# Seventeen expert products in fp32, dealt out through the choice of experts

## The chip, the cores and the metric

The kernel runs on one core of a Trainium2 chip. A core has TensorE (PE in the profile, with PEld for its weight loads), VectorE (DVE), ScalarE (ACT), GpSimd (POOL) and SyncE (SP), which here only issues transfers. The metric is the device time of one execution in microseconds.

## What is computed

Three transformer blocks stand behind one another, for 256 tokens of width 1024. The change lies in the first block, in a layer with 16384 small experts. Of the reference, this is what matters:

```python
def peer_ffn(h, w_q, sub_keys, u_tab, v_tab):          # h: 256 tokens x 1024
    q = (xt @ w_q).reshape(n_tok, 8, 2, 128)
    s = jnp.einsum('thpk,pnk->thpn', q, sub_keys)      # 8 heads x 2 halves x 128 keys
    top_s, top_i = lax.top_k(s, 16)
    cand_s = top_s[:, :, 0, :, None] + top_s[:, :, 1, None, :]   # 16 x 16 sums
    cand_i = top_i[:, :, 0, :, None] * 128 + top_i[:, :, 1, None, :]
    best_s, best_pos = lax.top_k(cand_s, 16)
    experts = take_along_axis(cand_i, best_pos)        # 16 experts per head and token
    gates = softmax(best_s)
    hid = gelu(einsum(u_tab[experts], x))              # one number per chosen expert
    return einsum(gates * hid, v_tab[experts])
...
e = (p @ ple_w_proj) * sigmoid(h @ ple_w_gate + ple_b_gate)
x = layer_norm(alpha * h + f + e)
```

## The kernel before

No expert is gathered. The kernel computes the up product of all 16384 experts for all tokens, weights the results with a coefficient that is zero for experts that a token did not choose, and multiplies by the whole down table. The up table is cut into 64 chunks of 256 experts (one transfer of 1 MB each), the down table likewise.

A product in this kernel is usually made of three matmuls in fp32r: the fp32 weight is split into `hi` (an ACT copy, line 319) and `lo` = weight - `hi` (a subtraction, line 320), the activations likewise, and `mm3` (lines 328 to 332) adds hi x hi, hi x lo and lo x hi. `wsplit` (line 308) loads a chunk into one of four `raw` buffers through SP's queue and splits it in two halves of 1024 columns. While `aside` is set, the subtraction goes to GpSimd and not to VectorE.

One up product, `Experts.up(j)` (line 943), takes one of two `mm` banks of PSUM: 2 x 8 times `mm3`, 48 matmuls, and a Gelu eviction into one of 18 `gel` tiles (line 951). Up products 0 to 17 can therefore run before any down product; each later one waits until `down` has freed a `gel`.

The stage `chosen` (line 855) runs in this order. Eight chunks of queries and scores give the sixteen best keys of each half (`top16`). Two up products follow, with their subtractions on GpSimd. Then `route` (line 779) is called for each of two tiles of 128 tokens: on VectorE it forms the 50 candidate sums that can matter, takes their sixteen best for each of 8 heads (lines 800 to 801), the softmax, and then, eight times, compares 16 positions with 50 candidates (`eq`, line 818), multiplies by the candidates' codes (line 820) and adds up (line 821). GpSimd forms the codes (lines 784 to 796). Three transposes on TensorE (`c.transpose`, line 469) and three ACT copies (line 831) put expert rows, columns and gates into `eT` and `gT`. `best`, `posf`, `ei` and `ef` have one buffer each, so the second tile's choice rewrites them only when the first one's transposes have read them.

The coefficient loop (lines 883 to 898) has 64 groups of four tokens. VectorE makes one `bm` (a one-hot of columns for four tokens, line 888) and four `am` (a one-hot of rows times the gate, line 894), TensorE multiplies them in fp32 into one PSUM bank (line 895), ACT evicts it into `stg` (line 896), and after every fourth group a transfer on ACT's queue writes `stg` to memory (line 898). Behind the loop stand up products 2 to 17 and `embed` (line 906): one chunk of the projection and four of the gate, again with `mm3`. The phase of the down products reads the coefficients back from memory as `slab` (line 959), multiplies them into `gel` (line 966), and adds into four `ac` banks.

The program order is not the order on the engines: a planner places each instruction by its own estimate of times, with earlier-written instructions first among those that are ready, and each engine then works through its queue in the planned order. Buffer waits follow from the numbers of buffers in the code.

Of the kernel before, what the change touches and what calls it, by code (L numbers as in the profile page):

```python
# [22 lines left out]
T = 256  # L23
# [4 lines left out]
WCH = 2048  # L28
HALFCH = 1024
GELS = 18  # L30
ASIDE_GELS = 2
ADDS = 4
LNV = 8
ASIDE = 100
EPS = (1e-6, 1e-5)
BASE = ("warm", "rs_v", "rs_r", "rs_t", "sqk", "yk", "sq2", "icol")

# [180 lines left out]
class Core:  # L218
    def __init__(self, tc, ctx, dram, vec_at):
        self.tc, self.nc, self.d = tc, tc.nc, dram  # L220
        nc = self.nc
        pool = lambda name, bufs, **k: ctx.enter_context(tc.tile_pool(name=name, bufs=bufs, **k))
        self.keep = pool("keep", 1)
        self.wp = pool("weights", 2)
        self.hn = pool("hn", 2)
        self.base = self.sm = pool("small", 2)
        self.pmm = pool("pmm", 2, space=PSUM)
        self.pac = pool("pac", 4, space=PSUM)
        self.pms = pool("pms", 2, space=PSUM)
        self.dr = pool("scratch", 1, space=DRAM)  # L230
        self.n = self.turn = self.aside = self.wide = 0
        self.kept = {}
        self.cst = self.keep.tile([128, CONST.n], F32, name="cst")
        nv = dram["vec"].shape[1]
        self.vecs = self.keep.tile([128, nv], F32, name="vecs")
        self.vec_at = vec_at
# [71 lines left out]
    def wsplit(self, src, rows, beside=()):  # L308

        nc = self.nc  # L310
        self.turn += 1
        eng = nc.gpsimd if self.aside and self.turn % self.aside else nc.vector
        raw = self.wraw(src, beside)
        n = src.shape[-1] // rows
        w = []
        for a in range(0, rows * n, HALFCH):
            m = min(HALFCH, rows * n - a)
            hi, lo = (self.wp.tile([128, HALFCH], F32R, tag=t, bufs=4, name=self.name(t))[:, :m] for t in ("hi", "lo"))
            nc.scalar.activation(hi, raw[:, a:a + m], AF.Copy)  # L319
            eng.tensor_tensor(lo, raw[:, a:a + m], hi, op=OP.subtract)  # L320
            w += [(hi[:, i:i + n], lo[:, i:i + n]) for i in range(0, m, n)]
        return w

# [454 lines left out]

def route(c, tt, tops, topi, eT, gT):

    nc = c.nc
    iota = c.C("iota")
    topf = c.small([16, 16], tag="topf", bufs=1)
    nc.gpsimd.tensor_copy(topf, topi)
    ts = tops.rearrange("p (h s) k -> p h s k", s=2)
    ti = topf.rearrange("p (h s) k -> p h s k", s=2)
    nc.gpsimd.tensor_scalar(ti[:, :, 0], ti[:, :, 0], 128.0, None, op0=OP.mult)
    cand = c.small([8, NCAND], tag="cand", bufs=1)
    code = c.small([8, NCAND], tag="code", bufs=1)
    for dst, src, eng in ((cand, ts, nc.vector), (code, ti, nc.gpsimd)):  # L790
        for i in range(8):
            o, n = OFFS[i], ROWS[i]
            eng.tensor_tensor(dst[:, :, o:o + n], src[:, :, 1, :n],
                              src[:, :, 0, i:i + 1].to_broadcast([128, 8, n]), op=OP.add)
        o = OFFS[8]
        eng.tensor_tensor(dst[:, :, o:], src[:, :, 0, 8:16], src[:, :, 1, 0:1].to_broadcast([128, 8, 8]), op=OP.add)
    best = c.small([8, 16], tag="best", bufs=1)
    posi = c.small([8, 16], U32, tag="posi", bufs=1)
    posf = c.small([8, 16], tag="posf", bufs=1)
    for i in range(8):  # L800
        top16(nc, best[:, i], posi[:, i], cand[:, i])
    nc.vector.tensor_copy(posf, posi)

    ga = best
    gs = c.small([8, 2], tag="gsum", bufs=1)
    top = c.small([8, 1], tag="gtop", bufs=1)
    nc.vector.tensor_copy(top, best[:, :, 0:1])
    nc.vector.tensor_tensor(ga, best, top.to_broadcast([128, 8, 16]), op=OP.subtract)
    nc.scalar.activation(ga, ga, AF.Exp)
    nc.vector.tensor_reduce(gs[:, :, 0:1], ga, axis=AX.X, op=OP.add)  # L810
    nc.vector.reciprocal(gs[:, :, 1:2], gs[:, :, 0:1])
    nc.vector.tensor_tensor(ga, ga, gs[:, :, 1:2].to_broadcast([128, 8, 16]), op=OP.mult)

    en = posf
    sh = [128, 16, NCAND]
    for i in range(8):
        eq = c.small([16, NCAND], tag="eq", bufs=2)
        nc.vector.tensor_tensor(eq, iota[:, None, :NCAND].to_broadcast(sh), posf[:, i, :, None].to_broadcast(sh),
                                op=OP.is_equal)
        nc.vector.tensor_tensor(eq, eq, code[:, i:i + 1].to_broadcast(sh), op=OP.mult)  # L820
        nc.vector.tensor_reduce(en[:, i], eq, axis=AX.X, op=OP.add)
    ei = c.small([2, 8, 16], I32, tag="ei", bufs=1)
    ef = c.small([2, 8, 16], tag="ef", bufs=1)
    nc.vector.tensor_copy(ei[:, 0], en)
    nc.vector.tensor_scalar(ei[:, 1], ei[:, 0], 127, None, op0=OP.bitwise_and)
    nc.vector.tensor_scalar(ei[:, 0], ei[:, 0], 7, None, op0=OP.logical_shift_right)
    nc.vector.tensor_copy(ef, ei)
    for src, dst in ((ef[:, 0], eT[:, 0]), (ef[:, 1], eT[:, 1]), (ga, gT)):
        ps = c.ms_ps()[:, :128]
        c.transpose(ps, src.rearrange("p a b -> p (a b)"))  # L830
        nc.scalar.activation(dst[:, tt * 128:tt * 128 + 128], ps, AF.Copy)
# [23 lines left out]
def chosen(c, h, hs, ex, scr):  # L855
# [9 lines left out]
    for j in range(8):  # L865
# [7 lines left out]
        for tt in range(2):  # L873
            nc.scalar.activation(sc[tt][:, 2 * j:2 * j + 2], ps[:, tt], AF.Copy)
            for i in (2 * j, 2 * j + 1):
                top16(nc, tops[tt][:, i], topi[tt][:, i], sc[tt][:, i])
    c.aside = ASIDE
    for j in range(ASIDE_GELS):
        ex.up(j)
    for tt in range(2):  # L880
        route(c, tt, tops[tt], topi[tt], eT, gT)
    c.aside = 0
    for tb in range(T // TB):
        stg = c.big([128, TB], nm="stg")
        for g in range(0, TB, 4):
            t0 = tb * TB + g
            bm = c.small([4, 128], tag="bm")
            nc.vector.tensor_tensor(bm, iota[:, None, :].to_broadcast([128, 4, 128]),
                                    eT[:, 1, t0:t0 + 4, None].to_broadcast([128, 4, 128]), op=OP.is_equal)
            ps = c.ms_ps()  # L890
            for i in range(4):
                am = c.small([128], tag="am", bufs=4)
                t = slice(t0 + i, t0 + i + 1)
                nc.vector.tensor_scalar(am, iota, eT[:, 0, t], gT[:, t], op0=OP.is_equal, op1=OP.mult)
                nc.tensor.matmul(ps[:, i * 128:i * 128 + 128], am, bm[:, i], start=True, stop=True)
            nc.scalar.activation(stg[:, :, g:g + 4].rearrange("p n t -> p t n"),
                                 ps.rearrange("p (t n) -> p t n", t=4), AF.Copy)
        nc.scalar.dma_start(scr[tb], stg.rearrange("p n t -> p (n t)"))
    c.aside = ASIDE
    for j in range(ASIDE_GELS, GELS):  # L900
        ex.up(j)
    embed(c, h, hs)
    c.aside = 0


def embed(c, h, hs):
# [8 lines left out]
    for j in range(4):  # L915
        pp = c.mm_ps().rearrange("p (f t) -> p f t", f=2)
        for k in range(2):
            for f in range(2):
                cs = slice((2 * j + f) * 128, (2 * j + f) * 128 + 128)
                c.mm3(pp[:, f], (w[k][0][:, cs], w[k][1][:, cs]), (pr[0][:, k], pr[1][:, k]), k + f == 0, k == 1,  # L920
                      skip_group_check=True)
        pe = c.small([2, T], tag="r2", bufs=6)
        nc.scalar.activation(pe, pp, AF.Copy)
        if j == 1:
            c.aside = 0
        pg = c.lin_chunk(d["w_pg"][j], hs)
        sg = c.small([2, T], tag="r2", bufs=6)
        for f in range(2):
            g = 2 * j + f
            nc.scalar.activation(sg[:, f], pg[:, f], AF.Sigmoid, bias=c.V("ple_b_gate")[:, g:g + 1])  # L930
        nc.vector.tensor_tensor(pe, pe, sg, op=OP.mult)
        x = h[:, 2 * j:2 * j + 2]
        nc.vector.scalar_tensor_tensor(x, x, alpha, pe, op0=OP.mult, op1=OP.add)


class Experts:
# [3 lines left out]
        self.c, self.h, self.hs, self.scr = c, h, hs, scr  # L940
        self.ys, self.gels, self.slabs = None, {}, {}

    def up(self, j):
        c, hs = self.c, self.hs
        w = c.wsplit(c.d["peer_u"][j], 2 * KT)
        ps = c.mm_ps().rearrange("p (f t) -> p f t", f=2)
        for i in range(2):
            for k in range(KT):
                c.mm3(ps[:, i], w[i * KT + k], (hs[0][:, k], hs[1][:, k]), k == 0, k == KT - 1)
        self.gels[j] = c.small([2, T], tag="gel", bufs=GELS)  # L950
        c.nc.scalar.activation(self.gels[j], ps, AF.Gelu)

    def down(self, j):
        c, nc = self.c, self.c.nc
# [34 lines left out]
def pad_heads(c, q):  # L989

    for hh in range(2):
        c.nc.gpsimd.memset(q[hh][HALF[1 - hh]], 0.0)


def skew(n, *steps):
# [1027 lines left out]
```

## Time and profile before

| | us |
|---|---|
| median of 3 runs | 3037.54 (3036.64 to 3039.58) |
| the profiled execution | 3037.25 |
| its span | 3035.1 |
| TensorE busy in the span | 2847.2 |
| VectorE busy | 2120.3 |
| ACT busy | 1580.2 |
| GpSimd busy | 271.9 |

A row of a timeline gives the start, the duration, the engine, the line, the operation with output and inputs, the shapes and how often it ran there; in brackets stands how long the engine had been idle and which instruction ended the wait. Consecutive instructions of one kind are merged into one row, whose duration then runs from the first start to the last end. Matmuls overlap, so their rate is read from the distance of their starts. The mean granted clock of TensorE in this execution is 0.959 of full speed.

### The profile page before, as it was taken

Reading aid. Unit: us, or ns where it says so; the run is one execution under the profiler, and the core shown is the slowest. Engines: PE = TensorE matmul, PEld = TensorE weight load, DVE = VectorE, ACT = ScalarE, POOL = GpSimd, SP = SyncE. Lnnn points to the kernel's source line nnn. Section 1 sums busy time; section 2 is a strip of 40 time slices with the busy share of each in tenths; the row PEclk is TensorE's granted clock in tenths of the full one; section 3 lists DMA queues with packets and bytes.
Section 4 is the critical chain, followed back from the end, with each engine's and each line's share of the span. In section 5 each row is a group of like instructions: output and inputs, shape, how many; then the busy total and the mean of one; then the engine's idle time right before and its main releaser. Section 6 shows DMA issues by size and latency. Waiting matters only on the chain. (4 is left out here: it accounts for less than half of the span.)

```text
span 3035.1 us, 52257 instructions
## 1 busy us (share of the span) xinstructions
PE 2847.2 (94%) x21378; PEld 2707.3 (89%) x21378; DVE 2120.3 (70%) x3619; ACT 1580.2 (52%) x2233; POOL 271.9 (9%) x176
## 2 busy tenths in 40 slices
PE   8799967899999999999999999999999999999998
PEld 8698966899999999988799988999899998788886
DVE  6365998976666667577655655555655596899997
ACT  5254534654444444436644455445544565777775
POOL 0000372200000000021000100000100062000000
PEclk9899988999999999999999999998999999999999
DMA  7544333477877788443155423543245442688885
GB/s 260 180 149 159 142 124 128 170 274 287 289 263 280 280 292 305 170 144 128 56 182 188 145 99 139 181 168 139 85 167 183 160 141 97 249 316 336 321 333 220
DMA packets 117712, 601.77 MB, mean 198 GB/s; under 512 B 9688, under 2 KB 45016, under 8 KB 48472
## 3 DMA queue, kind: packets, MB, share of 16 engines
q1 hardware_dynamic: 78480, 557.96, 50.5%
q10 hardware_dynamic: 38984, 40.39, 4.4%
q8 instruction: 170, 2.79, 0.4%
q14 instruction: 78, 0.64, 0.1%
HBM read 578.91 MB, written 19.39 MB: 197 GB/s over the span
## 5 line engine op out<-in xcount | busy, mean ns | idle before, releaser
L320 DVE TENSOR_TENSOR lo<-raw,hi 128x1024 fp32r<-128x1024 f32 x915 | 1123.5, 1244 | 601.6 <-ACT hi L319 598.4
L319 ACT ACTIVATE hi<-raw 128x1024 fp32r<-128x1024 f32 x955 | 1002.7, 1057 | 1021.1 <-PE mm L331 534.1
L330 PE MATMUL mm<-lhi,hi 128*128 128x256 f32 x1344 | 388.2, 289 | 5.5 <-ACT r L930 3.1
L332 PE MATMUL mm<-lhi,lo 128*128 128x256 f32 x1344 | 388.1, 289 | 3.6 <-DVE lo L320 3.5
L330 PE MATMUL mm<-nhi,hi 128*128 128x256 f32 x1312 | 378.8, 290 | 10.2 <-ACT nhi L494 6.8
L331 PE MATMUL mm<-llo,hi 128*128 128x256 f32 x1344 | 388.2, 289 | 0.0
L331 PE MATMUL mm<-nlo,hi 128*128 128x256 f32 x1312 | 379.0, 289 | 0.5 <-DVE nlo L495 0.5
L332 PE MATMUL mm<-nhi,lo 128*128 128x256 f32 x1312 | 376.8, 288 | 0.0
L330 PE MATMUL ac<-r,hi 128*128 128x256 f32 x1024 | 294.2, 288 | 0.7 <-ACT r L325 0.7
L331 PE MATMUL ac<-r,hi 128*128 128x256 f32 x1024 | 293.4, 287 | 0.0
L332 PE MATMUL ac<-r,lo 128*128 128x256 f32 x1024 | 293.2, 286 | 0.0
L330 PEld LDWEIGHTS mm<-lhi,hi 128*128 128x128 f32 x1344 | 262.3, 195 | 7.9 <-ACT r L930 3.7
L330 PEld LDWEIGHTS mm<-nhi,hi 128*128 128x128 f32 x1312 | 258.0, 197 | 12.3 <-ACT nhi L494 7.6
L332 PEld LDWEIGHTS mm<-lhi,lo 128*128 128x128 f32 x1344 | 262.5, 195 | 5.7 <-DVE lo L320 4.7
L331 PEld LDWEIGHTS mm<-llo,hi 128*128 128x128 f32 x1344 | 262.2, 195 | 1.1 <-issue 0.7
L331 PEld LDWEIGHTS mm<-nlo,hi 128*128 128x128 f32 x1312 | 257.9, 197 | 2.5 <-DVE nlo L495 1.7
L332 PEld LDWEIGHTS mm<-nhi,lo 128*128 128x128 f32 x1312 | 257.8, 197 | 0.1
L330 PEld LDWEIGHTS ac<-r,hi 128*128 128x128 f32 x1024 | 198.8, 194 | 0.9 <-ACT r L325 0.9
L331 PEld LDWEIGHTS ac<-r,hi 128*128 128x128 f32 x1024 | 198.8, 194 | 0.0
L332 PEld LDWEIGHTS ac<-r,lo 128*128 128x128 f32 x1024 | 198.3, 194 | 0.0
L331 PE MATMUL ac<-hlo,hi 128*128 128x256 f32 x688 | 193.0, 281 | 0.0
L330 PE MATMUL ac<-hhi,hi 128*128 128x256 f32 x688 | 192.8, 280 | 0.0
(591 smaller groups left out, 6253.6 us busy)
## 6 DMA issues: line engine op xcount, KB each, us to landing
raw<-in_moe_gu SPq DMA_DIRECT2D x88, 1024.0 KB, 5.9
raw<-in_peer_u SPq DMA_DIRECT2D x64, 1024.0 KB, 5.3
raw<-in_peer_v SPq DMA_DIRECT2D x64, 1024.0 KB, 4.9
raw<-in_ada SPq DMA_DIRECT2D x48, 1024.0 KB, 6.1
raw<-in_moe_d SPq DMA_DIRECT2D x40, 1024.0 KB, 5.9
raw<-in_up SPq DMA_DIRECT2D x32, 1024.0 KB, 4.9
raw<-in_down SPq DMA_DIRECT2D x32, 1024.0 KB, 4.9
raw<-in_ffn_gu SPq DMA_DIRECT2D x22, 1024.0 KB, 4.9
```

The lines of the kernel that those rows point to most:

```text
L319: nc.scalar.activation(hi, raw[:, a:a + m], AF.Copy)
L320: eng.tensor_tensor(lo, raw[:, a:a + m], hi, op=OP.subtract)
L330: mm(ps, w[0], x[0], start=start, stop=False, **k)
L331: mm(ps, w[0], x[1], start=False, stop=False, **k)
L332: mm(ps, w[1], x[0], start=False, stop=stop, **k)
```

## The change

The first seventeen up products no longer split their weights. Their matmuls take the raw fp32 weight and the unsplit fp32 activations: 16 matmuls for each product instead of 48, with neither `hi` nor `lo`. The eighteenth and all later ones are split as before. `aside` goes, so that every remaining subtraction runs on VectorE. The eighteen products become one sequence of 18 x 16 steps, which is dealt out: 16 steps ahead of the first `route`, 100 through each `route` (at its `yield`s: 5, 8 x 2, 8, 5, 8 x 7, 10), one with each of the 64 coefficient groups, and the rest behind the loop, ahead of `embed`. The loop's PSUM banks come from `ac` (four buffers) and not from `ms` (two), `bm` has three buffers instead of two and `am` eight instead of four.

```diff
     def wsplit(self, src, rows, beside=()):
-        self.turn += 1
-        eng = nc.gpsimd if self.aside and self.turn % self.aside else nc.vector
...
-            eng.tensor_tensor(lo, raw[:, a:a + m], hi, op=OP.subtract)
+            nc.vector.tensor_tensor(lo, raw[:, a:a + m], hi, op=OP.subtract)
...
 def route(c, tt, tops, topi, eT, gT):
...
+    yield 5
     for i in range(8):
         top16(nc, best[:, i], posi[:, i], cand[:, i])
+        yield 2
...
     nc.vector.tensor_tensor(ga, best, top.to_broadcast([128, 8, 16]), op=OP.subtract)
+    yield 8
     nc.scalar.activation(ga, ga, AF.Exp)
...
+    yield 5
...
         nc.vector.tensor_reduce(en[:, i], eq, axis=AX.X, op=OP.add)
+        yield 7
...
     nc.vector.tensor_copy(ef, ei)
+    yield 10
     for src, dst in ((ef[:, 0], eT[:, 0]), (ef[:, 1], eT[:, 1]), (ga, gT)):
...
-    c.aside = ASIDE
-    for j in range(ASIDE_GELS):
-        ex.up(j)
+    ups = chain.from_iterable(ex.steps(j, j < WHOLE) for j in range(GELS))
+    run(ups, 16)
     for tt in range(2):
-        route(c, tt, tops[tt], topi[tt], eT, gT)
-    c.aside = 0
+        for n in route(c, tt, tops[tt], topi[tt], eT, gT):
+            run(ups, n)
...
-            bm = c.small([4, 128], tag="bm")
+            bm = c.small([4, 128], tag="bm", bufs=3)
...
-            ps = c.ms_ps()
+            ps = c.ac_ps()
...
-                am = c.small([128], tag="am", bufs=4)
+                am = c.small([128], tag="am", bufs=8)
...
                                  ps.rearrange("p (t n) -> p t n", t=4), AF.Copy)
+            run(ups, 1)
...
-    c.aside = ASIDE
-    for j in range(ASIDE_GELS, GELS):
-        ex.up(j)
+    run(ups, 16 * GELS)
     embed(c, h, hs)
-    c.aside = 0
...
-    def up(self, j):
+    def steps(self, j, whole=False):
         c, hs = self.c, self.hs
-        w = c.wsplit(c.d["peer_u"][j], 2 * KT)
+        src = c.d["peer_u"][j]
+        w = c.wraw(src) if whole else c.wsplit(src, 2 * KT)
         ps = c.mm_ps().rearrange("p (f t) -> p f t", f=2)
         for i in range(2):
             for k in range(KT):
-                c.mm3(ps[:, i], w[i * KT + k], (hs[0][:, k], hs[1][:, k]), k == 0, k == KT - 1)
-        self.gels[j] = c.small([2, T], tag="gel", bufs=GELS)
-        c.nc.scalar.activation(self.gels[j], ps, AF.Gelu)
+                r = i * KT + k
+                if whole:
+                    c.nc.tensor.matmul(ps[:, i], w[:, r * 128:r * 128 + 128], self.h[:, k], start=k == 0,
+                                       stop=k == KT - 1)
+                else:
+                    c.mm3(ps[:, i], w[r], (hs[0][:, k], hs[1][:, k]), k == 0, k == KT - 1)
+                if r == 2 * KT - 1:
+                    self.gels[j] = c.small([2, T], tag="gel", bufs=GELS)
+                    c.nc.scalar.activation(self.gels[j], ps, AF.Gelu)
+                yield
+
+    def up(self, j):
+        run(self.steps(j), 2 * KT)
...
+def run(steps, n):
+    for _ in range(n):
+        next(steps, None)
```

## Rows read from the trace of the kernel before

**Rows 1.** The page's first part: busy time, share of the span, instructions.

```profile
PE   2847.2 (94%) x21378; PEld 2707.3 (89%) x21378; DVE 2120.3 (70%) x3619; ACT 1580.2 (52%) x2233; POOL 271.9 (9%) x176
```

**Rows 2.** Stretches: length; PE, PEld, DVE, ACT, POOL busy; granted clock; DMA share; GB/s.

```profile
358.20:639.00 280.80, 212.00 (x1615) 206.13 (x1613) 257.24 (x592) 136.68 (x158) 109.08 (x59) 0.88 0.41 151
...
411.30:466.00 54.70, 33.04 (x257) 32.84 (x258) 53.78 (x117) 17.63 (x22) 37.23 (x14) 0.78 0.33 116
466.00:612.00 146.00, 120.76 (x899) 116.61 (x899) 133.22 (x315) 85.09 (x91) 33.99 (x13) 0.93 0.41 159
612.00:639.00 27.00, 23.24 (x171) 22.23 (x171) 17.83 (x24) 13.30 (x21) 0.00 (x0) 0.94 0.72 239
```

**Rows 3.** Timeline of TensorE: the transposes at the end of each choice.

```profile
414.85 0.69 PE L469 MATMUL ms<-cst,ef 128*128 128x128 f32 x2 [21.58 <-DVE ef L827]
...
465.87 0.69 PE L469 MATMUL ms<-cst,ef 128*128 128x128 f32 x2 [18.11 <-DVE ef L827]
```

**Rows 4.** Timeline of VectorE and GpSimd in the second tile's choice.

```profile
423.45 1.89 DVE L818 TENSOR_TENSOR eq<-cst,posf 128x800 f32<-128x800 f32 x2
...
437.93 2.29 DVE L820 TENSOR_TENSOR eq<-eq,code 128x800 f32<-128x800 f32 x1
...
444.15 2.30 DVE L820 TENSOR_TENSOR eq<-eq,code 128x800 f32<-128x800 f32 x1
...
456.45 0.98 DVE L820 TENSOR_TENSOR eq<-eq,code 128x800 f32<-128x800 f32 x1
...
459.15 0.97 DVE L820 TENSOR_TENSOR eq<-eq,code 128x800 f32<-128x800 f32 x1
...
422.97 31.82 POOL L320 TENSOR_TENSOR lo<-raw,hi 128x1024 fp32r<-128x1024 f32 x10 [1.04 <-ACT hi L319]
```

**Rows 5.** Groups by line and shape, 363 to 640: busy us, mean ns.

```profile
L894 DVE TENSOR_SCALAR am<-cst,eT,gT 128x128 f32<-128x128 f32 x256 | 99.6, 443 | 12.5 <-PE ms L895 11.6
L895 PE MATMUL ms<-bm,am 128*128 128x128 f32 x512 | 80.3, 298 | 24.2 <-DVE am L894 24.1
...
L896 ACT ACTIVATE stg<-ms 128x512 f32<-128x512 f32 x64 | 66.9, 1068 | 58.1 <-PE ms L895 58.1
```

**Rows 6.** Timeline of TensorE: split matmuls, and two runs of fp32 matmuls.

```profile
389.15 0.28 PE L332 MATMUL mm<-lhi,lo 128*128 128x256 f32 x1
389.27 0.28 PE L330 MATMUL mm<-lhi,hi 128*128 128x256 f32 x1
...
510.21 2.08 PE L895 MATMUL ms<-bm,am 128*128 128x128 f32 x16
...
1308.44 3.62 PE L400 MATMUL ms<-x,cst 128*128 128x256 f32 x16
```

**Rows 7.** Timeline of VectorE and GpSimd in the coefficient loop.

```profile
541.85 3.19 DVE L894 TENSOR_SCALAR am<-cst,eT,gT 128x128 f32<-128x128 f32 x4 [0.92 <-PE ms L895]
...
565.63 0.68 DVE L888 TENSOR_TENSOR bm<-cst,eT 128x512 f32<-128x512 f32 x1
566.24 1.10 DVE L894 TENSOR_SCALAR am<-cst,eT,gT 128x128 f32<-128x128 f32 x4
567.27 0.67 DVE L888 TENSOR_TENSOR bm<-cst,eT 128x512 f32<-128x512 f32 x1
...
542.10 2.35 POOL L320 TENSOR_TENSOR lo<-raw,hi 128x1024 fp32r<-128x1024 f32 x1 [6.85 <-ACT hi L319]
```

**Rows 8.** The page's sixth part: transfers, KB each, median us to landing.

```profile
raw<-in_peer_u SPq DMA_DIRECT2D x64, 1024.0 KB, 5.3
```

**Rows 9.** Timeline around the loop's end: VectorE, ACT's queue, first down matmul.

```profile
610.32 1.22 DVE L320 TENSOR_TENSOR lo<-raw,hi 128x1024 fp32r<-128x1024 f32 x1
...
612.51 0.33 ACTq L898 DMA_DIRECT2D coef<-stg  x1
...
625.27 0.42 DVE L966 TENSOR_TENSOR gel<-gel,slab 128x256 f32<-128x256 f32 x1 [1.26 <-DMA slab<-coef]
...
639.00 0.74 PE L330 MATMUL ac<-r,hi 128*128 128x256 f32 x4 [0.74 <-ACT r L325]
```

More of the change, by code (lines that the diff above doesn't have):

```diff
@@ L30 @@
 GELS = 18
-ASIDE_GELS = 2
+WHOLE = 17
 ADDS = 4
 LNV = 8
-ASIDE = 100
 EPS = (1e-6, 1e-5)
@@ L230, in __init__ @@
         self.dr = pool("scratch", 1, space=DRAM)
-        self.n = self.turn = self.aside = self.wide = 0
+        self.n = self.wide = 0
         self.kept = {}
@@ L923, in embed @@
         nc.scalar.activation(pe, pp, AF.Copy)
-        if j == 1:
-            c.aside = 0
         pg = c.lin_chunk(d["w_pg"][j], hs)
```

## The prediction

> **What bounds the kernel now.** I read the engine totals of the page first: TensorE (PE) is busy for 94% of the span [rows 1], so only a stretch where PE lacks work can give much. The table by stage then shows the one that the change touches. It runs from PE's first up product (358.2 us) to the first matmul that adds into the four `ac` sums of the down products (639.00) [rows 2, 9]: 280.8 us, of which PE is busy 212.0, at a granted clock of 0.88. VectorE (DVE) is busy for 257.2 of them [rows 2]. So in this stage PE waits for DVE.
>
> How much of the 280.8 us is real PE work? In a run of split products the matmuls start 0.12 us apart [rows 6]. Eighteen products of 48 and the embedding's 240 (192 gates, 48 projections) are 1104 x 0.12 = 132.5 us. The coefficients' 256 fp32 matmuls are 512 instructions [rows 5]; a run of sixteen takes 2.08 us, so they too start 0.12 apart [rows 6]: 61.4 us. Six transposing instructions add 0.7. Together 194.6: about 86 us of the stage are lost.
>
> Where? Twice PE stands until DVE has finished a token tile's choice: 21.58 us before the transposes at 414.85 and 18.11 before those at 465.87 [rows 3]. The rest goes in the coefficient loop (25 us idle of 146, clock 0.93) and at the end (4 idle of 27) [rows 2], and in matmuls at the lower of the two clocks after each standstill.
>
> Why is DVE late? The timeline of DVE shows the same operation at two durations. The product with `code` (L820) takes 2.29 us while GpSimd (POOL) runs its ten subtractions without pause from 422.97 on, and 0.98 once these are over [rows 4]; the distance from one repeat to the next goes from 6.22 us (437.93 to 444.15) to 2.70 (456.45 to 459.15). In the loop a group of four `am` takes 3.19 us while POOL subtracts, against 1.10 [rows 7]. So POOL's subtractions, written to relieve DVE, hold it up.
>
> The Trainium skill ("SBUF — State Buffer", Two physically separate sides) says that a DVE operation with two SBUF inputs and a GpSimd operation that reads SBUF exclude each other for a whole instruction. The trace agrees: 2.29 against 0.98.
>
> **The change, part by part.**
>
> *Products in fp32.* Sixteen matmuls of two instructions each replace 48. The row for fp32 of 256 columns is the sum of rows at 1308.44: sixteen instructions in 3.62 us; the last lasts 0.379 as modelled, so they start (3.62 - 0.38) / 15 = 0.216 us apart [rows 6]. A step costs 0.432 us against 0.36, a product 6.91 against 5.76: seventeen cost PE 19.6 us more. That is the price.
>
> The Trainium skill ("FP8 and Floating Point Precision", TensorE Precision Notes) counts four passes for true fp32, against this change. Four times the 0.12 of a split matmul would be 0.48 a step, 0.048 above the row; over the 216 steps ahead of the loop the sum would end 10 us later. The row of this kernel decides for 0.432.
>
> *No splits.* 17 x 2 ACT copies and 17 x 2 POOL subtractions go; so do POOL's subtractions for the embedding's first two chunks, which return to DVE (4 x about 1.2 us, after the loop, where DVE has room: 17.8 busy of 27 [rows 2]). POOL keeps only the small `code` sums, some 3 us a tile. A raw buffer is now held for 6.9 us of products rather than for two copies; there are four, and a load lands in 5.3 us [rows 8], so none is awaited.
>
> *Order: 16 steps, 100 in each choice, 64 in the loop.* PE does 116 steps, 50.1 us, from 358.2 to 408.3. DVE needs for a choice what it took before its repeats in the second tile, 12.1 us (411.3 to 423.45), then 8 x 2.70 = 21.6 and some 2 at the end: 36 us [rows 2, 4]. It is ready near 400, so PE doesn't wait; DVE does, because `best` is rewritten only after its transpose. Transposes to 409; 100 steps, 43.2 us, and the second transposes to 453; DVE, at 445, waits again. Both waits are DVE's and hidden behind PE; were the steps fewer, PE would wait instead.
>
> *Loop.* With POOL quiet a group costs DVE 1.63 us (565.63 to 567.27) [rows 7], PE 8 x 0.12 + 0.432 = 1.39, ACT one 1.07 eviction [rows 5]. DVE is the bound. The new buffers (8 `am`, 3 `bm`, four `ac` banks instead of two) take away DVE's short waits for PE and let it run two groups ahead: 62 x 1.63 = 101.1 us and 2 x 1.2 for the eighteenth product's splits bring DVE to 556.5. PE idles some 15 us in gaps of a quarter microsecond; nothing fills them, as the embedding's splits come behind the `am` in DVE's queue, the way one already does at 610.32 [rows 9].
>
> *Tail.* One microsecond for the last group, the eighteenth product's remaining 8 steps (24 x 0.12 = 2.9), the embedding 28.8, the same 4 us of waits for its evictions as now, 1 us to the first `ac` matmul: 556.5 + 37.7 = 594.2. The coefficients' way through memory, from the last write (612.51) to the first use (625.27), is 12.8 us [rows 9]; it starts near 558 and ends near 571, behind the embedding. Without that cover it would cost its 12.8.
>
> The stage ends at 594 instead of 639: 45 us earlier. In work: 194.6 + 19.6 = 214.2 on PE, and 22 lost instead of 86. Behind the stage the code is the same. The profiled execution took 3037.25 us (span 3035.1), 0.3 under the median of 3037.54; 3037.5 - 45 = 2992.5.
>
> **The unknown costs.** (a) The fp32 step between 0.36, no dearer than a split one, and 0.45, an eighth of the whole 3.62 us [rows 6]: over the 216 steps 16 us earlier to 4 us later; I take 0.432, worked out from a row of the very shape. (b) Loop pace: from 1.39 (PE's own) to 2.28, the mean now (146 / 64 [rows 2]); I take 1.63, the pace when POOL is quiet. (c) The order: the instructions don't run as written but as a planner places them. The code writes two products ahead of the choice, which would end at 369.7, yet at 389.15 PE is at its sixth [rows 6]. So steps may be drawn forward.
>
> **Rivals.**
>
> 1. *Gaps filled.* The planner finds work for PE's gaps in the loop. PE then never stands: 358.2 + 214.2 + 4 = 576, which the coefficients' way (571 and 2 us of products and splits) just allows. Gain 63: 2974.5. For it: so it does now, where the projection runs before the loop's end. Against: the embedding's weights need DVE. 0.13.
>
> 2. *Steps run ahead.* The planner takes an fp32 step for cheaper than it is and places all 272 before the loop: 358.2 + 117.5 + 1.4 = 477; then the loop at DVE's pace with PE half empty, 477 + 103.5 + 37.7 = 618. Gain 21: 3016.5. For it: row at 389.15. Against: the dealt steps give PE written work all the time, so it has little cause to reach ahead. 0.14.
>
> 3. *DVE stays slow (the change doesn't do what it says).* If not POOL but something else stretches DVE (the loads, PE's own reads), the loop keeps its 146 us: choices at 51 us each to 466, loop to 612, tail to 648.7: 10 us slower, 3047. It decides from a pace of (639 - 37.7 - 466) / 64 = 2.1 us a group. Against: 0.98 returns as soon as POOL's row ends. 0.04.
>
> 4. *The fp32 stream at the lower clock.* If the chip grants 1.2 GHz through much of it, a step costs 0.86: all 272 would add 117 us, 3110; the gain is gone from a mean step of about 0.60. Against: the fp32 run at 1308.44 goes at 512 columns in 0.216 us, the full 2.4 GHz, and PE no longer stands before it. 0.03.
>
> **How the numbers follow.** Forecast 0.62, rivals as above, 0.04 for a schedule that I don't see. Range 2974 to 3014: from rival 1 through the forecast with (a) and a partial rival 2. Differences under about 0.2% (6 us) can't be told from none here. Faster: forecast, 1, 2 and half of the unseen, 0.91; same: the other half, 0.02; slower: 3 and 4, 0.07.
>
> **What would show it.** POOL's L320 gone; L820 at 0.98 and `am` at 0.34 (now 443 ns in the mean [rows 5]) throughout; up matmuls 0.216 apart; the waits of the transposes for `ef` gone from PE and DVE waiting there instead; loop groups 1.63 apart; the first `ac<-r` near 594; clock 1.0 from 358 on. I am wrong if PE still idles over 40 us in the stage, if L818 and L820 keep durations above 1 us, or if the loop starts later than about 465.

## The result, and the profile after

The changed kernel takes 2993.01 us (median of 4 runs, 2989.64 to 2994.33), the kernel before 3038.56 beside it on the same chip: a ratio of 0.9841 with a 95% interval of 0.9819 to 0.9863. The forecast was 2992.5. Two executions far from all others, one of the kernel before (7793.11 us) and one of e3 below (11125.55 us), are left out of the ratios.

In the trace the stage ends with the first `ac` matmul at 595.42, not at 639.00 [rows 9]: 43.6 us of the 47.2 by which the span is shorter (2987.9 against 3035.1). The remaining 3.6 us lie behind the stage, where the code is the same; from the first `ac` to the end the kernels of this study take 2386 to 2400 us, so differences of that size there mean nothing. For this reason the table of the experiments gives the time of the first `ac` beside the run's time.

The page's busy totals answer [rows 1]:

```profile
PE 2854.9 (96%) x21106; PEld 2699.0 (90%) x21106; DVE 2060.0 (69%) x3625; ACT 1547.6 (52%) x2199; POOL 160.8 (5%) x136
```

The table by stage of the changed kernel answers [rows 2] (length; PE, PEld, DVE, ACT and POOL busy; granted clock; DMA share; GB/s): the whole stage, the second choice, the coefficient loop, and what follows the last `am`.

```profile
355.42:595.42 240.00, 224.73 (x1383) 202.62 (x1382) 200.62 (x612) 109.95 (x130) 7.42 (x22) 0.99 0.53 189
406.00:450.00 44.00, 44.00 (x206) 38.51 (x206) 33.36 (x109) 7.18 (x12) 0.00 (x0) 1.00 0.45 159
450.00:553.50 103.50, 95.19 (x676) 86.09 (x675) 102.83 (x312) 73.03 (x77) 0.00 (x0) 1.00 0.54 207
553.50:595.42 41.92, 34.96 (x265) 33.53 (x265) 25.99 (x37) 19.52 (x27) 0.00 (x0) 0.92 0.73 245
```

PE is busy through the whole choice; in the loop DVE is busy 102.83 of 103.50; behind the loop neither is full. So three parts of the stage now have three different bounds. Over the whole stage PE stands still for 15.3 us (240.00 less 224.73), where it stood 68.8 before [rows 2]. POOL has 7.42 us left of 109.08.

The groups of DVE in 355 to 600 (busy us, mean ns of one, idle before) answer [rows 4, 5]. Line numbers are those of the changed kernel: its L820 (comparison) and L822 (product with `code`) are the lines 818 and 820 of the kernel before.

```profile
L897 DVE TENSOR_SCALAR am<-cst,eT,gT 128x128 f32<-128x128 f32 x256 | 71.3, 338 | 10.0 <-PE ac L898 10.0
L891 DVE TENSOR_TENSOR bm<-cst,eT 128x512 f32<-128x512 f32 x64 | 43.6, 682 | 11.8 <-ACT eT L835 11.8
...
L822 DVE TENSOR_TENSOR eq<-eq,code 128x800 f32<-128x800 f32 x16 | 15.7, 983 | 0.0
...
L820 DVE TENSOR_TENSOR eq<-cst,posf 128x800 f32<-128x800 f32 x16 | 15.6, 986 | 0.0
```

All 32 comparisons and products are at 0.98 us, `am` fell from 443 to 338 ns, and DVE now stands 21.8 us for what PE does (11.8 and 10.0) instead of PE for DVE. These are two single waits, one behind each choice (us in total, times, longest):

```profile
DVE bm L891 <- ACT eT L835: 11.8, 1, 11.8
DVE am L897 <- PE ac L898: 10.0, 1, 10.0
```

On PE's timeline the transposes have no wait in front of them, where [rows 3] show 21.58 and 18.11 us:

```profile
357.27 4.91 PE L953 MATMUL mm<-x,raw 128*128 128x256 f32 x22
...
406.48 0.38 PE L466 MATMUL ms<-cst,ef 128*128 128x128 f32 x2
...
450.02 0.38 PE L466 MATMUL ms<-cst,ef 128*128 128x128 f32 x2
...
521.23 1.17 PE L898 MATMUL ac<-bm,am 128*128 128x128 f32 x8 [0.46 <-DVE am L897]
522.86 1.17 PE L898 MATMUL ac<-bm,am 128*128 128x128 f32 x8 [0.46 <-DVE am L897]
...
540.95 0.38 PE L329 MATMUL mm<-lhi,lo 128*128 128x256 f32 x1 [0.64 <-DVE lo L317]
...
572.36 0.58 PE L329 MATMUL mm<-lhi,lo 128*128 128x256 f32 x1 [5.16 <-DVE lo L317]
...
595.42 0.64 PE L327 MATMUL ac<-r,hi 128*128 128x256 f32 x4
```

The first row gives the pace of the fp32 instructions, (4.91 - 0.38) / 21 = 0.216 us; a matmul is two of them. The rows at 521 and 522 show the loop late in its course: groups 1.63 apart, 0.46 us of standstill in each, and no up product between them. At 540.95 the eighteenth product goes on, once its split is there. The row at 572 is a wait that the prediction does not have.

### The profile page after: what moved, and what is told of

It reads as the page before. It is cut to its first block, busy times and chain, and to the rows that moved or that the text cites. A ratio compares the mean times of both kernels' runs of the same rounds, so it can differ in the third digit from the quotient of the medians.

```text
span 2987.9 us, 51592 instructions
## 1 busy us (share of the span) xinstructions
PE 2854.9 (96%) x21106; PEld 2699.0 (90%) x21106; DVE 2060.0 (69%) x3625; ACT 1547.6 (52%) x2199; POOL 160.8 (5%) x136
## 5 line engine op out<-in xcount | busy, mean ns | idle before, releaser
L316 ACT ACTIVATE hi<-raw 128x1024 fp32r<-128x1024 f32 x921 | 966.9, 1057 | 1001.6 <-PE mm L328 519.5
L329 PE MATMUL mm<-lhi,lo 128*128 128x256 f32 x1072 | 306.4, 286 | 8.3 <-DVE lo L317 8.3
L327 PE MATMUL mm<-lhi,hi 128*128 128x256 f32 x1072 | 305.9, 286 | 2.6 <-ACT lhi L454 2.3
L328 PE MATMUL mm<-llo,hi 128*128 128x256 f32 x1072 | 307.2, 287 | 0.0
L329 PEld LDWEIGHTS mm<-lhi,lo 128*128 128x128 f32 x1072 | 207.6, 194 | 10.5 <-DVE lo L317 9.5
L327 PEld LDWEIGHTS mm<-lhi,hi 128*128 128x128 f32 x1072 | 207.7, 194 | 4.4 <-ACT lhi L454 2.9
L328 PEld LDWEIGHTS mm<-llo,hi 128*128 128x128 f32 x1072 | 207.5, 194 | 1.1 <-issue 0.7
```

The lines of the kernel that those rows point to most:

```text
L327: mm(ps, w[0], x[0], start=start, stop=False, **k)
L328: mm(ps, w[0], x[1], start=False, stop=False, **k)
L329: mm(ps, w[1], x[0], start=False, stop=stop, **k)
```

## The experiments

Each ran beside the kernel before on its own chip, so the ratios compare across rows; a difference of two of them under about 0.003 is inside their intervals. The first and second transposes, the start of the last `am` and the first `ac` are from the profiled run of each.

| kernel | median us | ratio to before (95%) | transposes | last `am` | first `ac` |
|---|---|---|---|---|---|
| changed | 2993.01 | 0.9841 (0.9819 to 0.9863) | 406.48, 450.02 | 552.33 | 595.42 |
| e1 before, no GpSimd | 3048.76 | 1.0034 (1.0017 to 1.0052) | 400.99, 434.22 | 542.00 | 650.80 |
| e2 fp32, not dealt | 2991.53 | 0.9840 (0.9822 to 0.9857) | 396.24, 430.18 | 537.46 | 595.64 |
| e3 dealt, split | 3027.14 | 0.9968 (0.9951 to 0.9984) | 420.04, 474.73 | 595.62 | 626.46 |
| e4 idle GpSimd | 3004.77 | 0.9885 (0.9867 to 0.9903) | 409.55, 461.61 | 565.09 | 608.70 |
| e5 old buffers | 2993.78 | 0.9862 (0.9835 to 0.9889) | 406.57, 450.12 | 558.15 | 598.28 |
| e6 dealt anew | 2977.67 | 0.9799 (0.9780 to 0.9817) | 400.89, 437.52 | 540.66 | 583.72 |
| e7 late `gel` x `slab` | 2987.55 | 0.9832 (0.9815 to 0.9849) | 407.17, 450.71 | 552.95 | 592.40 |
| e8 e6 and e7 | 2975.31 | 0.9804 (0.9786 to 0.9822) | 401.17, 437.80 | 540.96 | 580.36 |
| e9 e2 and e7 | 2988.11 | 0.9831 (0.9810 to 0.9851) | 396.33, 429.93 | 537.39 | 591.78 |
| e10 e8, four split | 2979.11 | 0.9812 (0.9797 to 0.9827) | 404.43, 439.34 | 542.55 | 582.29 |
| e11 e8, nine fp32 | 2999.31 | 0.9866 (0.9846 to 0.9887) | 400.66, 440.81 | 554.46 | 598.93 |
| e12 e10, splits ahead | 2978.86 | 0.9807 (0.9786 to 0.9828) | 402.55, 438.40 | 541.58 | 581.23 |

### Which part of the change brings the time

**e1: the kernel before, with GpSimd's subtractions on VectorE.**

```diff
-        eng = nc.gpsimd if self.aside and self.turn % self.aside else nc.vector
+        eng = nc.vector
```

> The kernel before, with the subtractions of the split weights on VectorE instead of GpSimd: GpSimd rests, and nothing else is changed. My theory is that GpSimd's subtractions cost VectorE about as much by holding up its operations (some 50 us in the stage from 358 to 639: the choice's repeats at 6.2 us instead of 2.7, the groups of am at 3.2 instead of 1.1) as the 40 subtractions would cost on VectorE itself (40 x 1.15 = 46 us). Then moving them brings almost nothing: 3025 to 3045 us, L820 back to 0.98 us, VectorE still the bound. The rival, that GpSimd's rest alone carries the gain, expects 2990 to 3005. The rival that GpSimd has nothing to do with it expects VectorE's work to grow by 46 us: 3070 to 3085.

Slower by 0.34%, a little above the 3025 to 3045 us of the theory. DVE is relieved of the contention, as the groups of 363 to 640 show (line numbers of the kernel before):

```profile
L894 DVE TENSOR_SCALAR am<-cst,eT,gT 128x128 f32<-128x128 f32 x256 | 73.7, 375 | 0.2
...
L820 DVE TENSOR_TENSOR eq<-eq,code 128x800 f32<-128x800 f32 x16 | 15.7, 983 | 0.0
```

The choices end 13.9 and 31.6 us earlier than in [rows 3], the last `am` 67 us earlier than before. Yet the splits now stand behind the choice in DVE's queue and PE starves: in the stretches 355 to 405 and 405 to 450 it is busy 26.87 of 50 and 18.40 of 45 us.

```profile
355.00:405.00 50.00, 26.87 (x187) 25.32 (x187) 49.95 (x213) 15.48 (x21) 8.04 (x22) 0.75 0.20 69
405.00:450.00 45.00, 18.40 (x131) 17.71 (x130) 44.84 (x122) 13.88 (x17) 0.00 (x0) 0.67 0.13 47
```

The up products are then left for the time behind the loop (PE is busy 67.91 of the 70.80 us from 580 on), and the first `ac` comes at 650.80. A quiet GpSimd brings nothing while the splits stand on DVE instead; that they were put on ACT was not run.

**e2: fp32 products in the old order.** Two of the eighteen ahead of the choice, none in it or in the loop, the old numbers of buffers.

```diff
-    run(ups, 16)
+    run(ups, 32)
...
-            run(ups, n)
+            pass
...
-            run(ups, 1)
```

> The changed kernel without the dealing: the fp32 products stand where the split ones stood (two ahead of the choice, the rest behind the coefficient loop), with the loop's buffers of before (two banks, two bm, four am); GpSimd rests. My theory says that the gain comes from taking the splits away and that a planner that draws later work forward can fill TensorE by itself: 2985 to 3003 us. The rival, that the order by steps matters (TensorE stands before the transposes or late products pile up behind the loop), expects over 3008.

0.9840 against 0.9841: dealing and buffers, as written in the change, bring nothing that shows. The choices and the loop end 10 to 20 us earlier than in the changed kernel, because fewer products are in PE's queue ahead of the transposes (80 and 70 steps by the planner's own choice, against 116 and 100); then the products left for the end take that back, and the first `ac` falls within 0.2 us of the same place.

**e3: dealt out with the new buffers, all products split on GpSimd as before.** (`WHOLE = 0`, with `aside` as in the kernel before.)

> The changed kernel's dealing and buffers, but all eighteen products split as before, with the subtractions on GpSimd. My theory: GpSimd's subtractions still stretch VectorE's choice to about 50 us per tile, while the dealt steps cost only 0.36 us each on TensorE (116 steps 41.8 us, 100 steps 36 us), so TensorE stands before the transposes again: 3015 to 3040. The rival, that dealing alone brings the gain, expects 2985 to 3000.

0.9968. This is the other half of e2: with split weights the order is worth 0.3%, the unsplit weights 1.3 (with it) to 1.6% (without). The product with `code` takes 2048 ns in the mean and PE stands 19.92 and 15.84 us for `ef`, much as in [rows 3].

**e4: the changed kernel, with GpSimd kept busy.** Each fp32 product gets two subtractions whose result nobody reads.

```diff
+            for s in (0, HALFCH):
+                z = c.wp.tile([128, HALFCH], F32R, tag="lo", bufs=4, name=c.name("idle"))
+                c.nc.gpsimd.tensor_tensor(z, w[:, s:s + HALFCH], w[:, s:s + HALFCH], op=OP.subtract)
```

> The changed kernel, and GpSimd does again two subtractions of 128 x 1024 for each of the seventeen fp32 products, of the raw weight from itself, into a buffer that nobody reads. Nothing waits for them except the reuse of a raw buffer. My theory: VectorE's repeats in the choice go back from 0.98 to 2 or 3 us for L820 and L822, am groups from 1.10 to 3.2 where one overlaps; about 1.3 us for each of the 34, partly hidden behind TensorE in the choice: 3003 to 3025 us. The rival, that VectorE was slow for another reason (loads, TensorE's reads), expects the time of the changed kernel within 4 us, 2989 to 2998, and L820 and L822 at 0.98.

The first `ac` comes 13.3 us later, the run takes 12 us more. This is contention by itself: nobody waits for these results. The comparisons and products take half as long again in the mean, and DVE is busy without a pause from 405 to 450 (45.00 us). The first two rows are those of the kernel before (363 to 640), the last two those of e4:

```profile
L820 DVE TENSOR_TENSOR eq<-eq,code 128x800 f32<-128x800 f32 x16 | 31.1, 1956 | 0.0
L818 DVE TENSOR_TENSOR eq<-cst,posf 128x800 f32<-128x800 f32 x16 | 27.6, 1747 | 0.0
...
L820 DVE TENSOR_TENSOR eq<-cst,posf 128x800 f32<-128x800 f32 x16 | 24.0, 1510 | 0.0
L822 DVE TENSOR_TENSOR eq<-eq,code 128x800 f32<-128x800 f32 x16 | 23.9, 1496 | 0.0
```

The timelines of DVE and GpSimd show it in one place:

```profile
383.67 2.68 DVE L820 TENSOR_TENSOR eq<-cst,posf 128x800 f32<-128x800 f32 x1
386.27 0.97 DVE L823 TENSOR_REDUCE posf<-eq 128x16 f32<-128x800 f32 x1
387.17 1.78 DVE L822 TENSOR_TENSOR eq<-eq,code 128x800 f32<-128x800 f32 x1
...
390.67 0.97 DVE L822 TENSOR_TENSOR eq<-eq,code 128x800 f32<-128x800 f32 x1
...
383.15 4.95 POOL L951 TENSOR_TENSOR idle<-raw 128x1024 fp32r<-128x1024 f32 x2 [2.94 <-DMA raw<-in_peer_u]
```

The operations with two tensors take 2.68 and 1.78 us while GpSimd's two run, and 0.97 once they are over; the reduction between them, with one tensor, takes 0.97 either way. The Trainium skill ("SBUF — State Buffer", SBUF: two separate sides) names two kinds of DVE operation that exclude GpSimd's for a whole instruction: those with two SBUF inputs, if GpSimd's reads SBUF, and those in a two-port mode; the pair of L820 and L823 agrees with the first. `am`, which has one tensor and two columns of scalars as inputs, was stretched as well [rows 7]; whether it runs in such a mode no run here shows.

The delay arises in the choices (second transposes at 461.61, 11.6 us later, of 12.8 at the last `am`; PE stands 6.66 us for `ef` again), hardly in the loop, where few idle subtractions run:

```profile
461.61 0.69 PE L466 MATMUL ms<-cst,ef 128*128 128x128 f32 x2 [6.66 <-DVE ef L830]
```

### Which edits carry next to nothing

**e5: the changed kernel with the loop's old buffers** (`ms` 2, `bm` 2, `am` 4).

> The changed kernel with the loop's old buffers: two PSUM tiles of the small pool, two of bm, four of am. The theory of the prediction is that the loop goes by DVE at 1.63 us a group, so that more buffers ahead of it buy next to nothing: 0 to +8 us against the changed kernel's 2993.0, that is 2990 to 3001, with the last am between 552 and 560. The rival: the eight buffers of am let DVE run past the dealt steps that PE still has to do, and without them every dealt step stops DVE for its 0.43 us: 32 groups of up to 0.43 us, +8 to +14 us, that is 3001 to 3007.

2993.78, which can't be told from the changed kernel. In the trace the last `am` comes 5.8 us later and the first `ac` 2.9. The pace of a loop group stays 1.63; only where a dealt step stands between two groups does DVE pause (0.69 us at 503.80).

### What the changed kernel still leaves

**e6: fewer steps in the choice, more in the loop.** 84 steps through each choice instead of 100, and two steps instead of one in three of every four groups, all through the loop (`g` counts tokens, so `g < 12` is three groups of four; the expectation misstates this place).

```diff
-        yield 7
+        yield 6
...
-    yield 10
+    yield 2
...
-            run(ups, 1)
+            run(ups, 1 + (g < 12))
```

> The changed kernel with fewer steps in the choice (6 in place of 7 behind each of the lookups, 2 in place of 10 at its end) and one more in each of the first twelve groups of the loop of both blocks, so that the products last further into the loop. Theory (PE stands 0.46 us a group from 514.6 to 540 because the dealt steps are used up, about 7 us in all, and late groups have nothing to fill them): up to 7 us earlier for the last am and as much for the first ac, if the slab doesn't stop it: 2985 to 2990. Rival (the loop's end is set by DVE, and the tail by the slab's transfer behind the loop): last am up to 7 us earlier, yet the slab's wait starts as much earlier and PE then has less to do: 2990 to 2996.

2977.67, 15 us under the changed kernel (13 by the ratios) and twice what the theory gave; the first `ac` comes 11.7 us earlier. The expectation counted only PE's gaps in the loop. It left out that the loop is DVE's from its first group to its last, so that all of it moves with the transposes, which come 12.5 us earlier (437.52). The loop itself got no shorter: from the second transposes to the last `am` it takes 103.1 us, 102.3 in the changed kernel. In the stretches from 405 to 540 PE is full but for one microsecond, DVE but for 3.3:

```profile
405.00:450.00 45.00, 45.00 (x240) 40.38 (x239) 41.67 (x117) 14.33 (x19) 0.00 (x0) 1.00 0.42 146
450.00:480.00 30.00, 30.00 (x214) 28.41 (x213) 30.00 (x92) 20.11 (x21) 0.00 (x0) 1.00 0.62 237
480.00:510.00 30.00, 30.00 (x212) 28.35 (x210) 30.00 (x89) 22.80 (x24) 0.00 (x0) 1.00 0.64 228
510.00:540.00 30.00, 28.96 (x225) 27.63 (x224) 30.00 (x94) 22.30 (x23) 0.00 (x0) 1.00 0.63 251
540.00:560.00 20.00, 14.00 (x109) 13.03 (x108) 10.52 (x17) 8.69 (x11) 0.00 (x0) 0.94 0.67 231
```

**e7: the changed kernel, with the first eight multiplications of `gel` by `slab` queued on DVE behind the embedding.**

```diff
-            nc.vector.tensor_tensor(gi, gi, self.slabs[b][:, :, o + i], op=OP.mult)
+            if j < 4:
+                with c.tc.issue_after(self.last.ins):      # the embedding's last DVE operation
+                    nc.vector.tensor_tensor(gi, gi, self.slabs[b][:, :, o + i], op=OP.mult)
```

> The changed kernel, in which the first eight multiplications of gel by the slab are queued on DVE behind the embedding's last operation, so that no split for the embedding stands behind the slab's wait of 6.85 us. Theory (the tail is longer than forecast because the slab's way is not hidden: DVE stands for the slab and PE then 5.16 us for the split): 4 to 8 us less than the changed kernel, 2985 to 2989, with no wait of PE over 2 us between the last am and the first ac. Rival (PE is bound there by the evictions, and the wait only moves to the multiplications behind the embedding): 2991 to 2995, with the 5 us coming back as a wait ahead of the first matmul of the down products.

2987.55 is in the range of the theory, but the ratios (0.9832 and 0.9841) can't tell the two kernels apart. The trace can: the first `ac` comes 3.0 us earlier. In the changed kernel DVE stands in front of these multiplications, with the embedding's splits queued behind them:

```profile
553.35 4.61 DVE L317 TENSOR_TENSOR lo<-raw,hi 128x1024 fp32r<-128x1024 f32 x4
560.79 1.23 DVE L317 TENSOR_TENSOR lo<-raw,hi 128x1024 fp32r<-128x1024 f32 x1 [2.83 <-ACT hi L316]
568.87 0.76 DVE L978 TENSOR_TENSOR gel<-gel,slab 128x256 f32<-128x256 f32 x2 [6.85 <-DMA slab<-coef]
570.15 0.42 DVE L978 TENSOR_TENSOR gel<-gel,slab 128x256 f32<-128x256 f32 x1
571.09 1.22 DVE L317 TENSOR_TENSOR lo<-raw,hi 128x1024 fp32r<-128x1024 f32 x1
```

In e7 PE's 5.16 us are gone, and 2.10 of them come back as a wait for the down product's own operand, as the rival had it for all five:

```profile
592.40 0.73 PE L327 MATMUL ac<-r,hi 128*128 128x256 f32 x4 [2.10 <-ACT r L322]
```

**e8: e6 and e7 together.**

> The dealing of e6 and the late multiplications of e7 together. In e6 the last am comes at 541.8, DVE then stands 6.65 us for the slab, and PE 5.0 us for a split behind it. Theory (the two losses are separate: one of the loop, one of the order of DVE's queue): 4 to 7 us less than e6's 2977.7, 2970 to 2974, with PE over 16 of the 20 us of 540 to 560 (14.0 in e6). Rival (the evictions of the down products take the stand over, as the 2.1 us wait for r ahead of the first ac in e7): 2975 to 2979.

The rival was nearer: 2975.31, which can't be told from e6 by the ratios (0.9804 and 0.9799). PE is busy 18.38 us of 540 to 560 where e6 has 14.00, so the edit does what it says; in the trace the first `ac` comes 3.4 us earlier, again with a wait for `r` (2.08 us) in front of it. A gain of 3 us can't be seen in the time.

**e9: e2 with the late multiplications.**

> The kernel of e2 (fp32 products in the old order of the program, not dealt, the loop's old buffers), with the first eight multiplications of gel by the slab queued on DVE behind the embedding's last operation. In e2 the last am came at 538, 15 us ahead of the changed kernel's, and DVE then stood 17.24 us for the slab. Theory (that stand is what e2 loses again, since the embedding's splits are queued behind it): 10 to 17 us less than e2, 2974 to 2982. Rival (products that are left for behind the loop keep PE busy up to the slab anyway, so that only what PE stood in e2 behind DVE comes back): 2984 to 2990.

The theory falls: 2988.11 lies in the rival's range, and its ratio can't be told from that of e2. DVE's 17.24 us for the slab in e2,

```profile
556.94 0.43 DVE L977 TENSOR_TENSOR gel<-gel,slab 128x256 f32<-128x256 f32 x1 [17.24 <-DMA slab<-coef]
```

were not PE's: products left for the end fed PE all but 4.83 us of that time, and the first `ac` gains 3.9 us. DVE's standstill was mostly covered.

### Whether split products are cheaper somewhere

**e10: e8, products 2 to 5 split.**

```diff
-    ups = chain.from_iterable(ex.steps(j, j < WHOLE) for j in range(GELS))
+    ups = chain.from_iterable(ex.steps(j, j < WHOLE and not 2 <= j < 6) for j in range(GELS))
```

> The kernel of e8, in which the products 2 to 5 keep their split (hi on ACT, lo on DVE, two operations of 1.22 us each), so that their 16 steps are three fp32r passes each and not one fp32 matmul of 0.432 us. They fall in the choice, where PE is busy all the time and DVE in e6 stood 8.5 of 82 us. Theory (unsplit costs PE 1.15 us a product, as the prediction has it, and DVE has room in the choice): PE 4.6 us less, DVE 9.8 us more of which the 8.5 us take most: 0 to 5 us less than e8, 2967 to 2973. Rival (the splits stand behind the choice in DVE's queue, as in e1, and starve PE): 3 to 15 us more than e8, 2975 to 2987.

No gain: 0.9812 beside 0.9804. PE saves its passes and loses 3.44 us in one wait for a split in the first choice:

```profile
393.87 0.39 PE L329 MATMUL mm<-lhi,lo 128*128 128x256 f32 x1 [3.44 <-DVE lo L317]
```

**e12: the same, each of the four splits given out a product ahead.**

```diff
+        if 1 <= j < 5:
+            self.ws[j + 1] = c.wsplit(c.d["peer_u"][j + 1], 2 * KT)
```

> The kernel of e10 (products 2 to 5 split), in which each of the four splits is given out a whole product ahead of its steps, some 7 us of PE's time. In e10 PE was busy 45.90 of the 50 us of 355 to 405 and the transposes of the first choice came at 404.43, 3.3 us later than in e8. Theory (DVE has room for four splits in the choice, and e10 lost its gain only because each split stood in DVE's queue behind the choice): PE stands no more, the first transposes come at 398 to 401, and the time is 2 to 5 us under e8's 2975.3, that is 2970 to 2973. Rival (DVE's 9.8 us of splits lengthen the choice by as much, wherever they stand, since DVE had but 8 us of waits there): transposes at 403 to 406, the time 2975 to 2981.

The waits for the splits are gone from the choice, and the same time stands elsewhere:

```profile
402.55 0.69 PE L466 MATMUL ms<-cst,ef 128*128 128x128 f32 x2 [4.87 <-DVE ef L830]
```

The rival was nearer: the time lies in its range, the transposes (402.55) between the two ranges. The order of DVE's queue was not what e10 lacked: the splits, 8 x 1.22 = 9.8 us, lengthen the first choice past PE's work. Even four of seventeen splits turn the first choice back into a stretch where PE waits for DVE.

**e11: e8, the last nine products split** (`j < 9`).

> The kernel of e8 with nine products in fp32 and the last nine split. Those fall mostly in the loop, where DVE in e6 was busy 103.6 of 105 us. PE has 8 times 1.15 = 9.2 us less, DVE 16 splits of 1.22 us = 19.5 us more. Theory (in the loop DVE sets the time, so a product's split there costs DVE's whole time and its PE saving is worth nothing): 8 to 20 us more than e8, 2979 to 2991. Rival (PE's total sets the time, since the tail can take what the loop leaves): 3 to 9 us less than e8, 2962 to 2969.

24 us more, beyond the expectation of 8 to 20; 18.6 of them lie ahead of the first `ac`. The last `am` is 13.5 us later: 3.0 of them are lost in the second choice (transposes at 440.81 instead of 437.80), 10.5 in a loop where DVE is busy without pause (30.00 of 30.00 us from 450 to 480, from 480 to 510 and from 510 to 540). Behind it another 5 us are lost, with a wait of 7.86 us for `r` in front of the first `ac` (2.08 in e8). In these runs a split is dearest where DVE is the bound.

## Why the prediction was right, and where its steps were not

**The bound and its cause.** Right. Without GpSimd's subtractions L820, L822 and `am` have their short durations; e4 puts back a part of the contention by itself (L820 and L822 at 1.51 and 1.50 us in the mean, where the kernel before has 1.75 and 1.96) and gives back 12 of 45 us. How the rest divides between contention and the splits' own work no run shows. e1 shows that on DVE the splits cost at least what the contention did: only without both is there a gain (e2 and the changed kernel).

**The fp32 step.** 0.432 us, as taken from [rows 6]: two instructions of 0.216 us. The four passes that the Trainium skill ("FP8 and Floating Point Precision", TensorE Precision Notes) counts would be 0.48 at 0.12 each, an estimate. The measured 0.432 decides against that price and not against the count: four passes of 0.108 us would fit it as well.

**The choices.** The transposes came at 406.48 and 450.02, not 409 and 453: the first up product began at 355.42 and not at 358.2, with its first steps ahead of the last scores. From there the 116 and the 100 steps took what was forecast (51.1 and 43.5 us). DVE waits for PE, as said, though not in the place that was named: the instruction that stands is not a rewriting of `best` but the loop's first `bm`, for `eT`, and then an `am` two groups further on. DVE was ready at 395.5 and 440.6, some 4 us before the forecast, which changed nothing, as PE set the time. But "were the steps fewer, PE would wait instead" was too strong. In e6 there are sixteen fewer in each choice, PE waits for nothing there, and the loop starts 12.5 us earlier. DVE's 21.8 us of waits, which the prediction called hidden behind PE, were hidden from PE; they delayed the loop, where DVE is the bound.

**The loop.** 1.63 us a group, right; the last `am` ended at 553.4 against 556.5, as much ahead as the choice. The gaps were said to be a quarter microsecond each throughout. In fact the planner drew the fp32 steps forward: the last stands before 512, PE is full until 514, and then has 0.46 us a group with nothing to fill it until 540.95. What could fill it is the eighteenth product, but its splits come only at 539.69, behind the `am` in DVE's queue. Rival 2 was right in part about the mechanism (steps run ahead, though within the loop and not all ahead of it) and wrong about its price, since PE is not the bound there. The short waits that the buffers were said to take away come to 2.9 us at the first `ac` (e5), too little to show in the time.

**The tail.** Here a term was mis-sized: 42.0 us from the last `am` to the first `ac`, not 37.7. The failed step is "the coefficients' way through memory ... ends behind the embedding". The embedding's matmuls would have covered it. Its splits could not, as they stand behind the `gel` x `slab` multiplications in DVE's queue: DVE waits 6.85 us for the slab, PE then 5.16 for a split, and the granted clock falls to 0.83 in 560 to 580. With the order turned round (e7) the first `ac` comes 39.5 us behind the start of the last `am`, and not 43.1. Another part of the term is not there at all: the eighteenth product's 2.9 us, since it ended in the loop's gaps (its Gelu stands at 551.7); 22 matmuls of the next up product, 2.6 us, take that place. The prediction looked for what PE had left to do, and not for what was queued behind the waiting instruction.

**The sum.** The choice 3 us early and the tail 4 us late cancel to 1.2 us at the first `ac` (595.42, forecast 594.2). That the total was right within 0.5 us is partly luck; each term was right within 5 us. None of the signs of being wrong appeared: PE idles 15.3 us, the comparisons and products stay under 1 us, and the loop starts at 450.

**The rivals.** Rival 1, PE's gaps filled, had 2974.5. The change does not reach it. e6 and e8 come near its time (2977.67 and 2975.31) by the number of steps given to each part, but by another way: PE's gaps are filled and the loop is no shorter; it only starts earlier. Rival 3 falls with the comparisons and products at 0.98; its tail would end at 649.7 and not 648.7 (612 + 37.7), on which nothing rests. Rival 4 falls with a granted clock of 0.99 in the stage (0.88 before).

## What to carry to other kernels

Before work is given to GpSimd to relieve VectorE, compare the duration of the same VectorE operation with GpSimd busy and idle. Here it doubled, and the relief brought next to nothing: giving the work back to VectorE cost 0.34% (e1). Taking the work away, at 1.2 times the matmul time (0.432 us a step for 0.36), brought 1.6%. When products are dealt out to fill another engine's time, count per stage which engine is the bound: a step too many in the stage that PE bounds delays the stage that DVE bounds (e6: 15 us for moving 32 steps). For every wait on a transfer, read what stands behind the waiting instruction in its engine's queue.

## What was unexpected of the hardware

The distance between two records is not always a pace. In the changed kernel's loop the first split matmul behind an fp32 group has 0.20 us to the next, against 0.12 within a run, as if the change of type cost time:

```profile
511.71 1.05 PE L898 MATMUL ac<-bm,am 128*128 128x128 f32 x8
512.52 0.36 PE L327 MATMUL mm<-lhi,hi 128*128 128x256 f32 x1
512.72 0.28 PE L328 MATMUL mm<-llo,hi 128*128 128x256 f32 x1
512.84 0.28 PE L327 MATMUL mm<-r,hi 128*128 128x256 f32 x1
```

It cost none here: from 511.71 to 512.72 are nine starts in 1.01 us, 0.112 each. The first split matmul's start is early in the record.

Nor is the mean duration of a short DVE operation a pace: in e4 four `am` last 1.22 us around 543, in the changed kernel 1.10, at the same distance of 1.63 us from group to group. The 375 ns of e1 beside 338 are of this kind.
